# A third seven-product group in the second layer's feed-forward part, with its weight sums made during the first layer's

## The chip, the cores and the metric

The kernel runs on one core of one Trainium2 chip. The metric is the device time of one execution in microseconds; three executions of the kernel before took 783.09, 784.54 and 783.81 us, with a median of 783.81 us. The profile is of a further execution that took 783.19 us.

## The reference

The program is a decoder of two layers over 256 tokens of width 1024, in float32. Layer 0 mixes tokens by a short gated convolution, layer 1 by block-sparse attention on one shared set of keys and values; both then attend to a memory of 256 rows, and both end in a gated feed-forward part of width 2816. That part is what the change is about:

```
D_FF = ((8 * D_MODEL + 3 * 256 - 1) // (3 * 256)) * 256   # 2816

def swiglu(h, w_gu, w_down):
    g, u = jnp.split(h @ w_gu, 2, axis=-1)
    return (jax.nn.silu(g) * u) @ w_down

# in each layer, h of 256 x 1024:
x = x + swiglu(rms_norm(x, norm_ffn), w_gu, w_down)
```

## The kernel before

**Weights.** All matrix products are float32 made of two rounded halves: a weight chunk of 512 KB arrives as `raw_...`, ScalarE rounds it to `hi_...` (the hi split), VectorE subtracts that from the chunk to make `lo_...` (the lo split), and TensorE (`mm3`) forms lo x hi, hi x hi and hi x lo. The chunks have one fixed order, the plan of 278 loads. `RAWS = 5`: a load is issued on SyncE's queue as soon as the chunk five places before it has its lo split. `WBUFS = 10`: ten split chunks may stand ready or in use.

**The feed-forward part.** The 2816 columns are 11 pairs `jp` of 256. Pairs 0 and 1 are made another way. A plain pair loads two gate chunks `wg{l}_{jp}`, two up chunks `wu{l}_{jp}` and the two chunks of down weights `wd{l}_{k}` of the pair two places back. TensorE forms gate and up in PSUM (`gu`) for half of the tokens, ScalarE and VectorE evict them (COPY and addition into `gu_sb`, SiLU, product) into `guT`, and TensorE adds the down products of the earlier pair into `ff`; then the second half of the tokens follows. The stages that the prediction speaks of in layer 0 are pair 6, whose stage uses wd0_8 and wd0_9, and pair 7 with wd0_10 and wd0_11.

**A group** (`seven`) makes two pairs at once. Gate and up of two pairs are seen as a 2 x 2 block of matrices, and seven products of blocks take the place of eight. The products read, in this order, B11, B21, the sums T1, T4, T2, then B22 and T3, two chunks each, with the down products of the earlier pairs put in between. The evictions of the products combine them: B11 by a ScalarE COPY into `m1`; B21 by a VectorE addition into `g0`, then SiLU on ScalarE; T1 by a ScalarE COPY into `p5` and a VectorE subtraction in `m1`; T4, T2, B22 and T3 by VectorE. The result lies with tokens on partitions and is turned by eight transposes (`turn_parts4`, PSUM tile `pt_g`), four for each half of the tokens, the second four while the stage behind the group is running.

**The sums.** T1 to T4 are sums of weight blocks, made in DRAM ahead of their use: for each chunk a copy on SyncE's queue and an accumulating transfer issued by GpSimd (`sum_steps`, eight copies and eight accumulates a group). Their place is given by load numbers: a sum step is issued just before the load of that number. [...]

**What sets the order.** The order of instructions on ScalarE and VectorE is set when the program is built, by a model of a clock. Each time TensorE's work reaches a poll, `poll` takes the open evictions whose inputs the model holds ready, and `pump` issues the next hi or lo split if its engine and its input are free by the model. Loads, copies and accumulates are all charged to one DMA clock, 3300 ns for an accumulate and 1460 for a copy, and a chunk counts as landed by this clock. Once built, the order is fixed: an engine that waits for one instruction doesn't do the next one.

`GROUPS` (L46) lists the first pair of each group by layer, and L47 the load numbers for the sums: first, end and last for each layer. The hooks that put them in are at L1041 to L1046.

```
GROUPS = ((8,), (4, 8))
SUMS_AT = ((44, 104, 104), (128, 220, 210))
```

## Time and profile before

| | |
|---|---|
| median of three runs | 783.81 us |
| the profiled execution | 783.19 us |
| its span | 781.4 us, 11230 instructions |
| granted clock of TensorE, mean | 0.998 |
| lo splits of down chunks on VectorE | 44 x 1.219 us |
| hi splits of down chunks on ScalarE | 44 x 1.050 us |
| read from HBM, written | 178.82 MB, 28.31 MB |

The page gives busy time by engine, then the span in 40 slices, the DMA queues, the chain of work that ended last, the costliest groups of instructions and the DMA issues. Where it names times in a row of the timeline, the first number is the start in us from the span's start and the second the duration; a row that ends in `x4` puts four like instructions together, and brackets hold the idle time ahead of it and what ended that. A row of the windows has the stretch, its length, the busy time of TensorE's matmuls (with the count), of its weight loads, VectorE, ScalarE and GpSimd, then TensorE's granted clock, the busy share of the DMA engines and GB/s.

### The profile page before, as it was taken

What the parts mean: (1) busy time and instruction counts of PE and PEld (TensorE: products, weight loads), DVE (VectorE), ACT (ScalarE), POOL (GpSimd) and SP (SyncE); (2) the same over time, 40 slices, a digit from 0 to 9 for tenths busy, and PEclk for the clock granted to TensorE, in tenths of its full rate; (3) what the DMA queues carried; (4) which work ended last, traced back from release to release, by engine and by line L of the source; (5) the groups of instructions that cost most, each with busy time, mean ns of one, the idle gap of its engine ahead of it and who ended that gap; (6) DMA issues with size and microseconds to landing.
All of it is one profiled execution on the core that took longest, in us unless ns stands there. A gap on an engine that the chain in (4) does not pass through costs nothing.

```text
span 781.4 us, 11230 instructions
## 1 busy us (share of the span) xinstructions
PE 773.5 (99%) x4147; PEld 664.8 (85%) x4147; DVE 574.0 (73%) x872; ACT 459.0 (59%) x728; POOL 39.1 (5%) x68
## 2 busy tenths in 40 slices
PE   9999999999999999999999999999999999999996
PEld 8988888898888888888888889888988888888885
DVE  6988887768785566688756566876867876966964
ACT  7875666665654555566654563655756556655741
POOL 1000011000100000000100010020001000000000
PEclk9999999999999999999999999999999999999999
DMA  9876888926676755699788466889975646946921
GB/s 343 299 259 212 272 292 267 336 65 212 188 247 235 223 177 204 206 367 346 211 251 295 178 161 210 302 239 300 247 209 166 240 159 216 330 165 210 348 107 54
DMA packets 53415, 182.71 MB, mean 234 GB/s; under 512 B 6256, under 2 KB 7280, under 8 KB 52720
## 3 DMA queue, kind: packets, MB, share of 16 engines
q1 hardware_dynamic: 45968, 166.79, 60.0%
q0 software_dynamic: 6816, 14.68, 10.4%
q8 instruction: 32, 0.52, 0.3%
q10 hardware_dynamic: 576, 0.52, 0.2%
q14 instruction: 23, 0.19, 0.1%
HBM read 178.82 MB, written 28.31 MB: 265 GB/s over the span
## 4 chain that ended last, share of the span: by engine, by line
PE 98%; DVE 1%; issue 0%; ACT 0%; POOLq 0%; DVEq 0%; ACTq 0%
PE gu L464 17%; PE ff L464 15%; PE seven L464 7%; PE acc_memk L464 6%; PE q_acc L464 6%; PE cu L464 6%; PE rows L464 6%; PE acc_mo L464 6%; PE acc_memv L464 6%; PE pb L464 3%; PE acc_v L464 3%; PE acc_q L464 3%; PE acc_o L464 3%; PE acc_cout L464 3%; PE acc_k L464 3%; PE po L464 2%
## 5 line engine op out<-in xcount | busy, mean ns | idle before, releaser
L464 PE MATMUL ff<-hi_wd,guT 128*128 128x512 f32 (+1 forms) x352 | 108.3, 388 | 0.0
L464 PEld LDWEIGHTS ff<-hi_wd,guT 128*128 128x128 f32 x352 | 65.8, 188 | 12.8
L464 PE MATMUL ff<-lo_wd,guT 128*128 128x512 f32 (+1 forms) x176 | 68.3, 388 | 0.0
L242 DVE TENSOR_TENSOR gu_sb<-gu_sb,gu 128x256 f32<-128x256 f32 x48 | 19.9, 420 | 57.5 <-ACT gu_sb L242 57.0
L242 DVE TENSOR_TENSOR lo_wd<-raw_wd,hi_wd 128x1024 fp32r<-128x1024 f32 x44 | 53.4, 1219 | 3.7 <-ACT hi_wd L242 3.6
L242 ACT COPY gu_sb<-gu 128x256 f32<-128x256 f32 x48 | 17.8, 373 | 60.0 <-PE gu L464 59.6
L242 ACT CAST hi_wd<-raw_wd 128x1024 fp32r<-128x1024 f32 x44 | 46.1, 1050 | 11.3 <-DMA raw_wd<-in_chunks_dram 11.0
L464 PE MATMUL gu<-ffn,hi_wg 128*128 128x512 f32 x192 | 48.0, 390 | 0.0
L464 PE MATMUL gu<-ffn,hi_wu 128*128 128x512 f32 x192 | 47.6, 390 | 0.0
L464 PE MATMUL acc_memk<-mT,hi_memk 128*128 128x256 f32 x256 | 44.3, 291 | 0.0
L242 ACT CAST hi_wu<-raw_wu 128x1024 fp32r<-128x1024 f32 x32 | 33.6, 1052 | 17.3 <-DMA raw_wu<-in_chunks_dram 12.6
L464 PEld LDWEIGHTS gu<-ffn,hi_wg 128*128 128x128 f32 x192 | 35.9, 188 | 7.3
L464 PEld LDWEIGHTS gu<-ffn,hi_wu 128*128 128x128 f32 x192 | 35.8, 188 | 7.3
L464 PE MATMUL rows<-hi_wr,ffn 128*128 128x512 f32 x128 | 40.7, 395 | 0.0
L464 PE MATMUL acc_mo<-hi_mo,oT_mem 128*128 128x512 f32 x128 | 40.6, 393 | 0.0
L242 DVE TENSOR_TENSOR lo_wu<-raw_wu,hi_wu 128x1024 fp32r<-128x1024 f32 x32 | 38.8, 1219 | 1.3 <-ACT hi_wu L242 1.2
L464 PE MATMUL acc_memv<-hi_memv,mT 128*128 128x512 f32 x128 | 39.6, 390 | 0.0
L464 PEld LDWEIGHTS acc_memk<-mT,hi_memk 128*128 128x128 f32 x256 | 38.7, 197 | 0.6 <-ACT hi_memk L242 0.4
L464 PEld LDWEIGHTS ff<-lo_wd,guT 128*128 128x128 f32 x176 | 33.2, 188 | 6.3
L551 POOL DMA_DIRECT2D T<-in_chunks_dram x24 | 21.9, 913 | 271.4 <-issue 92.1
L242 POOL TENSOR_TENSOR rs<-ms,neg_half 128x1 f32<-128x1 f32 x14 | 13.4, 960 | 395.5 <-DVE ms L242 386.3
L464 PE MATMUL q_acc<-mem,hi_mq 128*128 128x512 f32 x128 | 32.4, 394 | 0.0
(277 smaller groups left out, 1963.8 us busy)
## 6 DMA issues: line engine op xcount, KB each, us to landing
raw_wd<-in_chunks_dram SPq DMA_DIRECT2D x44, 512.0 KB, 5.1
raw_wu<-in_chunks_dram SPq DMA_DIRECT2D x32, 512.0 KB, 5.0
T<-in_chunks_dram POOLq DMA_DIRECT2D x24, 512.0 KB, 8.6
raw_wg<-in_chunks_dram SPq DMA_DIRECT2D x24, 512.0 KB, 5.2
raw_wT<-T SPq DMA_DIRECT2D x24, 512.0 KB, 4.8
raw_wB<-in_chunks_dram SPq DMA_DIRECT2D x18, 512.0 KB, 4.8
raw_memv<-in_chunks_dram SPq DMA_DIRECT2D x16, 512.0 KB, 5.0
raw_mq<-in_chunks_dram SPq DMA_DIRECT2D x16, 512.0 KB, 5.1
```

The costliest lines, as they stand in the source:

```text
L242: return call(out, *args, **kw)
L464: nc.tensor.matmul(o, l, r, start=start, stop=stop)
L551: nc.gpsimd.dma_start(dst, src, accum_op=OP.add, max_dma_last_dim=2048)
```

## The change

There are three groups in layer 1 instead of two, at pairs 3 and 4, 6 and 7, 8 and 9 (before: 4 and 5, 8 and 9). Pairs 2, 5 and 10 stay plain. The last two groups follow each other with no plain pair between them. The plan grows from 278 to 284 loads, since a group reads 14 chunks where two pairs read 8. TensorE's matmuls go from 4103 to 4067.

A group that starts at an odd pair has its two pairs in two different units of `guT`, so `turn_parts4` puts its four turned columns into two units, by two shorter COPYs and subtractions each instead of one.

The places of the sums are now listed by hand, one load number for each step. The sums of layer 0's group (8) stay where they were, and those of layer 1's groups 6 and 8 stand at the numbers that groups 4 and 8 had. New are the sums of group 3, at loads 94 to 116: in layer 0's feed-forward part, from the load of wd0_6 to that of wT4_0_8_0.

The descriptor space goes from 1024 to 2048 bytes a partition; the room comes from `junk` and `blank`, which have one buffer instead of two.

```diff
-GROUPS = ((8,), (4, 8))
-SUMS_AT = ((44, 104, 104), (128, 220, 210))
+GROUPS = ((8,), (3, 6, 8))
+SUMS_AT = {
+    (0, 8): (44, 47, 51, 55, 59, 62, 66, 70, 74, 77, 81, 85, 89, 92, 96, 100),
+    (1, 3): (94, 95, 97, 98, 100, 101, 107, 108, 103, 104, 106, 107, 111, 112, 115, 116),
...
+}
...
-        junk = small.tile([P, 512], BF16, tag="junk", name="junk", bufs=2)
+        junk = small.tile([P, 512], BF16, tag="junk", name="junk", bufs=1)
...
-        steps = [step for jp in GROUPS[l] for step in sum_steps(l, jp)]
-        first, end, last = SUMS_AT[l]
-        for n, step in enumerate(steps):
-            at = min(first + (end - first) * n // len(steps), last + n - len(steps))
-            feed.hooks.setdefault(at, []).append(step)
+        for jp in GROUPS[l]:
+            for at, step in zip(SUMS_AT[l, jp], sum_steps(l, jp)):
+                feed.hooks.setdefault(at, []).append(step)
...
-                yield from split_steps(u[:, :, 0, tok(h)], u[:, :, 1, tok(h)], pt)
+                if j0 == 0:
+                    yield from split_steps(u[:, :, 0, tok(h)], u[:, :, 1, tok(h)], pt)
+                    return
+                for i, v in enumerate((u, unit_of(2 * jp + 2)[0])):
+                    c, q = slice(2 - 2 * i, 4 - 2 * i), pt[:, 2 * i:2 * i + 2, :]
+                    scalar.copy(v[:, c, 0, tok(h)], q)
+                    yield
+                    vector.tensor_sub(v[:, c, 1, tok(h)], q, v[:, c, 0, tok(h)])
+                side.give("tp")
+                yield
...
-                guT.add_job(h, jp // 2, bank_jobs[name])
+                for g in sorted({jp // 2, (jp + 1) // 2}):
+                    guT.add_job(h, g, bank_jobs[name])
...
-    nc = bacc.Bacc("TRN2", target_bir_lowering=False, num_devices=1, dynamic_dma_scratch_size=1024)
+    nc = bacc.Bacc("TRN2", target_bir_lowering=False, num_devices=1, dynamic_dma_scratch_size=2048)
```

The change moves instructions in layer 0 too, where nothing of the computation is changed. Line numbers of the changed kernel are 5 higher there (L247 for L242).

The first place is ScalarE's queue around the hi split of wd0_9, in layer 0's pair 6. Before, it stands ahead of all evictions of that pair; `gu_3092` and `gu_3104` are gate and up of pair 5's second half, and pair 6's gate product is `gu_3160`.

```order
L242 COPY gu_sb0_3090<-gu_3092 128x256
L242 CAST hi_wd0_8_3129<-raw_wd0_8_3022 128x1024
L242 COPY gu_sb1_3091<-gu_3104 128x256
L242 ACTIVATE gu_sb0_3090<-gu_sb0_3090 128x256
L242 CAST hi_wd0_9_3146<-raw_wd0_9_3033 128x1024
L242 CAST guT0_2_2858<-gu_sb1_3091 128x256
L242 CAST hi_wg0_7_0_3165<-raw_wg0_7_0_3044 128x1024
L242 CAST hi_wg0_7_1_3175<-raw_wg0_7_1_3056 128x1024
L242 CAST hi_wu0_7_0_3187<-raw_wu0_7_0_3095 128x1024
L242 CAST hi_wu0_7_1_3207<-raw_wu0_7_1_3153 128x1024
L242 COPY gu_sb0_3158<-gu_3160 128x256
```

In the changed kernel ScalarE has this order there; `gu_3171` and `gu_3183` are gate and up of pair 6's first half, which TensorE forms just before it uses wd0_8 and wd0_9.

```order
L247 CAST hi_wd0_8_3165<-raw_wd0_8_3035 128x1024
L247 COPY gu_sb0_3169<-gu_3171 128x256
L247 CAST hi_wd0_9_3208<-raw_wd0_9_3044 128x1024
L247 COPY gu_sb1_3170<-gu_3183 128x256
L247 ACTIVATE gu_sb0_3169<-gu_sb0_3169 128x256
```

The hi split of wd0_9 has moved behind the COPY of pair 6's own gate product, and the chunks of pair 7, which were split ahead of that COPY, follow later.

The second place is the same queue one pair later, around the hi split of wd0_11. Before, `gu_3241` and `gu_3253` are gate and up of pair 6's second half, so that this split too stands a half stage and more ahead of pair 7's evictions.

```order
L242 COPY gu_sb0_3239<-gu_3241 128x256
L242 CAST hi_wd0_10_3278<-raw_wd0_10_3171 128x1024
L242 COPY gu_sb1_3240<-gu_3253 128x256
L242 ACTIVATE gu_sb0_3239<-gu_sb0_3239 128x256
L242 CAST hi_wd0_11_3295<-raw_wd0_11_3182 128x1024
```

In the changed kernel `gu_3320` and `gu_3329` are gate and up of pair 7's first half.

```order
L247 CAST hi_wd0_10_3331<-raw_wd0_10_3216 128x1024
L247 COPY gu_sb0_3318<-gu_3320 128x256
L247 COPY gu_sb1_3319<-gu_3329 128x256
L247 CAST hi_wd0_11_3364<-raw_wd0_11_3237 128x1024
L247 ACTIVATE gu_sb0_3318<-gu_sb0_3318 128x256
```

The hi split of wd0_11 now stands behind both COPYs of pair 7's first half, whose products TensorE forms just before it uses wd0_10 and wd0_11.

The third place is layer 0's group, on VectorE: `lo_w...` are lo splits, and the rows with `seven` are the evictions of B21 (into `g0`), T1 and T2 (into `m1`) and T4 (into `p5`). Before:

```order
L242 TENSOR_TENSOR lo_wT1_0_8_0_3461<-raw_wT1_0_8_0_3341,hi_wT1_0_8_0_3460 128x1024
L242 TENSOR_TENSOR lo_wT1_0_8_1_3471<-raw_wT1_0_8_1_3353,hi_wT1_0_8_1_3470 128x1024
L242 TENSOR_TENSOR lo_wT4_0_8_0_3482<-raw_wT4_0_8_0_3392,hi_wT4_0_8_0_3481 128x1024
L242 TENSOR_TENSOR lo_wT4_0_8_1_3502<-raw_wT4_0_8_1_3450,hi_wT4_0_8_1_3501 128x1024
L242 TENSOR_TENSOR lo_wT2_0_8_0_3509<-raw_wT2_0_8_0_3466,hi_wT2_0_8_0_3508 128x1024
L242 TENSOR_TENSOR g0_3526<-seven_3495,m1_3484 128x512
```

And in the changed kernel:

```order
L247 TENSOR_TENSOR lo_wT1_0_8_0_3510<-raw_wT1_0_8_0_3417,hi_wT1_0_8_0_3509 128x1024
L247 TENSOR_TENSOR g0_3523<-seven_3501,m1_3487 128x512
L247 TENSOR_TENSOR lo_wT1_0_8_1_3540<-raw_wT1_0_8_1_3461,hi_wT1_0_8_1_3539 128x1024
L247 TENSOR_TENSOR m1_3487<-seven_3532,m1_3487 128x512
L247 TENSOR_TENSOR lo_wT4_0_8_0_3561<-raw_wT4_0_8_0_3475,hi_wT4_0_8_0_3560 128x1024
...
L247 TENSOR_TENSOR lo_wd0_15_3614<-raw_wd0_15_3565,hi_wd0_15_3613 128x1024
L247 TENSOR_TENSOR m1_3487<-seven_3607,m1_3487 128x512
L247 TENSOR_TENSOR lo_wB22_0_8_0_3627<-raw_wB22_0_8_0_3580,hi_wB22_0_8_0_3626 128x1024
```

The eviction of B21 stood behind five lo splits of sums and now stands between the two of T1; the evictions of T1 and T2 now stand just ahead of the lo splits of wT4_0_8_0 and wB22_0_8_0.

ScalarE's queue shows the same in the changed kernel; `m1`, `g0` and `p5` are the COPY of B11, the SiLU on B21's sum and the COPY of T1.

```order
L247 CAST hi_wB21_0_8_0_3482<-raw_wB21_0_8_0_3369 128x1024
L247 COPY m1_3487<-seven_3467 128x512
L247 CAST hi_wB21_0_8_1_3497<-raw_wB21_0_8_1_3403 128x1024
L247 CAST hi_wT1_0_8_0_3509<-raw_wT1_0_8_0_3417 128x1024
L247 ACTIVATE g0_3523<-g0_3523 128x512
L247 CAST hi_wT1_0_8_1_3539<-raw_wT1_0_8_1_3461 128x1024
L247 COPY p5_3551<-seven_3532 128x512
L247 CAST hi_wT4_0_8_0_3560<-raw_wT4_0_8_0_3475 128x1024
```

Before, the hi splits of these chunks (of wB21 the second, of T1 both, of T4 the first) all stand ahead of that COPY of B11:

```order
L242 CAST hi_wB21_0_8_1_3443<-raw_wB21_0_8_1_3330 128x1024
L242 CAST guT0_3_3157<-gu_sb1_3388 128x256
L242 CAST hi_wT1_0_8_0_3460<-raw_wT1_0_8_0_3341 128x1024
L242 CAST hi_wT1_0_8_1_3470<-raw_wT1_0_8_1_3353 128x1024
L242 CAST hi_wT4_0_8_0_3481<-raw_wT4_0_8_0_3392 128x1024
L242 COPY m1_3484<-seven_3455 128x512
```

Each of the four hi splits after the first row has changed places with an eviction of the same group.

## The prediction

> **What bounds the kernel now.** The page comes first: how busy each engine is, which clock was granted, what the DMA queues carried, and the chain of work that ended last.

> ```profile
> PE   773.5 (99%) x4147; PEld 664.8 (85%) x4147; DVE 574.0 (73%) x872; ACT 459.0 (59%) x728; POOL 39.1 (5%) x68
> ...
> PEclk9999999999999999999999999999999999999999
> ...
> q1 hardware_dynamic: 45968, 166.79, 60.0%
> q0 software_dynamic: 6816, 14.68, 10.4%
> ...
> PE 98%; DVE 1%; issue 0%; ACT 0%; POOLq 0%; DVEq 0%; ACTq 0%
> ...
> raw_wd<-in_chunks_dram SPq DMA_DIRECT2D x44, 512.0 KB, 5.1
> ...
> T<-in_chunks_dram POOLq DMA_DIRECT2D x24, 512.0 KB, 8.6
> ```

> TensorE is busy in 773.5 of 781.4 us, at full clock in every slice, and makes up 98% of the chain. So only two things move the time much: matrix work that is added or removed, and stalls of TensorE where today there are none. VectorE (73%) and ScalarE (59%) have room on average, yet every weight chunk passes both of them (the hi split on ScalarE, then the lo split on VectorE) before TensorE may use it. A split that comes too late is the way in which this kernel can lose.

> **Part 1: the third group on TensorE.** The window view below cuts layer 1's feed-forward part where TensorE starts each stage: plain jp 3, the group of 4 and 5, plain jp 6, plain jp 7, the group of 8 and 9.

> ```profile
> 634.91:651.48 16.57, 16.57 (x89) 14.35 (x88) 10.10 (x15) 8.52 (x15) 0.00 (x0) 1.00 0.58 191
> 651.48:682.34 30.86, 30.86 (x138) 25.18 (x136) 28.53 (x31) 22.27 (x25) 0.00 (x0) 1.00 0.92 318
> 682.34:699.40 17.06, 17.06 (x94) 14.74 (x92) 9.79 (x14) 7.93 (x15) 0.00 (x0) 1.00 0.49 164
> 699.40:715.97 16.57, 16.57 (x89) 14.35 (x88) 10.05 (x15) 8.47 (x15) 0.00 (x0) 1.00 0.55 190
> 715.97:746.83 30.86, 30.86 (x137) 25.18 (x136) 28.47 (x31) 22.26 (x25) 0.00 (x0) 1.00 0.91 321
> ```

> Two plain pairs take 2 x 16.57 = 33.14 us, a group 30.86 us. Its result needs turning by eight transposes, four of which fall into the stage behind it: 17.06 instead of 16.57, 0.49 us. One more group thus saves 33.14 - 30.86 - 0.49 = **1.79 us**. This is sure as far as the group stays bound by TensorE, as both present ones do (busy 30.86 of 30.86).

> Two groups now stand back to back. VectorE is busy 28.5 of a group's 30.86 us, ScalarE 22.3, the DMA engines 0.91 to 0.92. A second group behind the first needs the same again, and the first one's last turning, some 1 us of VectorE; 2.3 us are free in each. I charge nothing; the cover is thin, and rival C prices its loss. The single unit that an odd group start now splits over two units costs two short ScalarE copies and two short VectorE subtractions for one long one each, a fraction of a microsecond off TensorE's path: nothing. [...]

> **Part 2: what the eight new sums do to the order in layer 0.** This is the term that decides. The planner charges each copy and accumulate to its DMA clock, so from the load of wd0_6 on it believes the next chunks to land later. It therefore hands ScalarE and VectorE the evictions first and the splits behind them, and the engines run in that order even if the chunk has long landed. The pieces of order shown above have the places: an eviction waits for the end of a TensorE product, and the split queued behind it feeds the matmuls that come almost directly after that product. Before, these splits were far ahead. The timelines of the three engines show it for wd0_9:

> ```profile
> 291.20 1.22 DVE L242 TENSOR_TENSOR lo_wd<-raw_wd,hi_wd 128x1024 fp32r<-128x1024 f32 x1
> ...
> 295.52 0.37 ACT L242 COPY gu_sb<-gu 128x256 f32<-128x256 f32 x1 [0.24 <-PE gu L464]
> ...
> 296.93 0.40 PE L464 MATMUL ff<-lo_wd,guT 128*128 128x512 f32 x1
> ...
> 329.94 1.05 ACT L242 CAST hi_wT<-raw_wT 128x1024 fp32r<-128x1024 f32 x1 [1.41 <-DMA raw_wT<-T]
> ...
> 331.02 1.23 DVE L242 TENSOR_TENSOR lo_wT<-raw_wT,hi_wT 128x1024 fp32r<-128x1024 f32 x1 [0.91 <-ACT hi_wT L242]
> ...
> 335.95 0.58 ACT L242 COPY p<-seven 128x512 f32<-128x512 f32 x1
> 336.43 2.00 ACT L242 CAST hi_wB<-raw_wB 128x1024 fp32r<-128x1024 f32 x2
> ```

> The lo split of wd0_9 ended at 292.42, 4.5 us ahead of its use at 296.93. Two steps are read here for all chains. From the start of a hi split to the end of its lo split: 329.94 to 331.02 + 1.23, **2.31 us**. And ScalarE starts the next operation 0.10 us before a COPY's recorded end (335.95 + 0.58 against 336.43), so 0.27 us after the start of a 0.37 us COPY and 0.48 after that of a 0.58 us one.

> All times below are on the clock of the old trace; a stall moves what follows, but the distance from a product to the use behind it stays, so the stalls add up.

> (1) wd0_9 now stands behind the COPY of its own stage's gate product, which starts at 295.52. Hi split from 295.79, lo done 298.10, use 296.93: **1.17 us**.

> (2) wd0_11 stands behind both COPYs of its stage, the second reading the up product:

> ```profile
> 295.27 1.12 PE L464 MATMUL gu<-ffn,lo_wu 128*128 128x256 f32 x8
> ...
> 296.49 0.37 ACT L242 COPY gu_sb<-gu 128x256 f32<-128x256 f32 x1 [0.59 <-PE gu L464]
> ...
> 311.84 1.12 PE L464 MATMUL gu<-ffn,lo_wu 128*128 128x256 f32 x8
> ...
> 313.50 0.40 PE L464 MATMUL ff<-lo_wd,guT 128*128 128x512 f32 x1
> ```

> In the stage before, that COPY starts 1.22 us after the first of the product's last eight matmuls. Here: 311.84 + 1.22 = 313.06, hi from 313.33, lo done 315.64, use 313.50: **2.14 us**.

> (3) wB21_0_8_1 stands behind the COPY of product B11, (4) wT1_0_8_1 behind the SiLU of product B21, which itself waits for VectorE's addition, and (5) wT4_0_8_0 behind the COPY of product T1, (6) wB22_0_8_0 on VectorE alone behind the addition that reads T2.

> ```profile
> 326.76 0.59 ACT L242 COPY m<-seven 128x512 f32<-128x512 f32 x1 [0.37 <-PE seven L464]
> ...
> 334.49 0.63 ACT L242 ACTIVATE g<-g 128x512 f32<-128x512 f32 x1
> 335.02 1.03 ACT L242 CAST hi_wd<-raw_wd 128x1024 fp32r<-128x1024 f32 x1
> ...
> 343.70 0.68 DVE L242 TENSOR_TENSOR m<-seven,m 128x512 f32<-128x512 f32 x1
> 344.31 1.22 DVE L242 TENSOR_TENSOR lo_wg<-raw_wg,hi_wg 128x1024 fp32r<-128x1024 f32 x1
> ```

> ```profile
> 326.10 0.62 PE L464 MATMUL seven<-hi_wB,ffn 128*128 128x512 f32 x2
> ...
> 329.28 0.39 PE L464 MATMUL seven<-lo_wB,ffn 128*128 128x512 f32 x1
> ...
> 330.18 0.62 PE L464 MATMUL seven<-hi_wB,ffn 128*128 128x512 f32 x2
> ...
> 333.41 0.39 PE L464 MATMUL seven<-lo_wT,S 128*128 128x512 f32 x1
> ...
> 334.34 0.63 PE L464 MATMUL seven<-hi_wT,S 128*128 128x512 f32 x2
> ...
> 336.19 0.40 PE L464 MATMUL seven<-lo_wT,ffn 128*128 128x512 f32 x1
> ...
> 342.63 0.63 PE L464 MATMUL seven<-hi_wT,S 128*128 128x512 f32 x2
> ...
> 343.79 0.39 PE L464 MATMUL ff<-lo_wd,guT 128*128 128x512 f32 x1
> ...
> 344.48 0.40 PE L464 MATMUL seven<-lo_wB,S 128*128 128x512 f32 x1
> ```

> (3) COPY 326.76, hi 327.24, lo done 329.55, use 329.28: **0.27**. (4) B21 ends at 330.80; an eviction starts about 0.05 behind a product's recorded end (B11: 326.10 + 0.62 against 326.76), so the addition runs 330.85 to 331.53, the SiLU starts at 331.58, the hi split 0.53 later at 332.11, lo done 334.42, use 333.41: **1.01**. (5) T1 ends at 334.97, COPY 335.02, hi 335.50, lo done 337.81, use 336.19: **1.62**. (6) T2 ends at 343.26, addition 343.31, the next operation 0.61 later at 343.92, lo done 345.14, use 344.48: **0.66**.

> Together 1.17 + 2.14 + 0.27 + 1.01 + 1.62 + 0.66 = **6.87 us** of new stalls. Bounds: if the present lead of several microseconds survived in some way, 0; if the hi split also started a whole eviction later at each place, by 0.4 to 0.7 us, about 10. I take the sum as it stands, since every step has its own row.

> **The sum.** -1.79 + 6.87 = +5.08 us. The profiled execution took 783.19 us, so the like would take 788.3; against the median of 783.81 it is 788.9. I say **788.6 us**.

> **Rivals.** A, the other side: not slower. The new order may not bind, because the evictions finish earlier against the product than I read (matmul ends are modelled in this profile). Against the median the change is no longer slower by 0.2%, which is what a measurement of this kernel can tell from no change (1.57 us), once the six stalls sum to less than 1.79 + 1.57 = 3.36 us, half of mine; each would have to be about 0.6 us shorter. With none at all the gain alone remains: 783.81 - 1.79 = 782.0, just past that bound. For it speaks that no stall of this kind is in the old trace; against it that the starts of the COPYs are measured. Chance 0.16, of which 0.06 is for faster.

> B: the chunks really land late. A queue's share of the span gives the price of a transfer: q0 10.4% of 781.4 us over 24 accumulates, at most 3.4 us each; q1 60.0% over 166.79 MB, 1.47 us for 512 KB. Eight copies and eight accumulates are 8 x 4.87 = 39 us of DMA time, between the loads of wd0_6 and the group's. There the windows show:

> ```profile
> 300.00:315.00 15.00, 15.00 (x83) 13.04 (x82) 8.66 (x13) 8.52 (x14) 0.00 (x0) 1.00 0.52 175
> 315.00:330.00 15.00, 15.00 (x76) 12.71 (x75) 9.76 (x12) 7.71 (x12) 0.00 (x0) 1.00 0.52 178
> 330.00:345.00 15.00, 15.00 (x67) 12.21 (x66) 12.64 (x14) 10.09 (x11) 0.00 (x0) 1.00 0.97 340
> ```

> Half of the time is free until 330, then nothing. A load takes the buffer of the chunk five places before it, so wd0_15 can now be issued only when lo_wT4_0 is done, at TensorE's stall of place (5); from there to its first use TensorE has about 7.6 us of work (336.19 to 343.79), and landing 5.1 plus splits 2.31 need 7.4. A landing as long as that of an accumulate, 8.6 us, would cost up to 3.5 us. In the forecast I take 0, by the nearest row, the median landing of 5.1; this rival adds 2 to 4: 791 to 793. Chance 0.18. [...]

> C: the two groups back to back run out of VectorE or DMA (28.5 of 30.86 and 0.92 above). Price: the shortfall of one turning and one late chunk, 1 to 3 us, 789.6 to 791.6. Chance 0.07.

> **How the numbers follow.** My forecast 0.59 (787 to 790.5), A 0.16, B 0.18, C 0.07. The range 785.0 to 793.0 leaves out most of A and the far end of B. Faster than 782.2: 0.06; between 782.2 and 785.4: 0.11; above: 0.83.

> **What would show it.** In the new trace TensorE should wait, at weight loads or matmuls, for VectorE's lo splits of wd0_9, wd0_11, wT1_0_8_1, wT4_0_8_0 and wB22_0_8_0, some 7 us in all, and nowhere else in such amounts; ScalarE should be idle ahead of the COPYs in front of those splits, with the chunks landed. Layer 1's feed-forward part should be 1.8 us shorter with TensorE busy throughout. I am wrong in mechanism if these waits end on a DMA, or if layer 0 takes as long as before.

## The result and the profile after

The changed kernel took 792.22 us in the median of five runs (790.75 to 793.95), against 783.38 us before in the same comparison: 1.12% slower, ratio 1.0112 with a 95% interval of 1.0093 to 1.0130. The profile is of the fastest of the five: 790.75 us with a span of 789.0 us, 7.6 us more than the span before.

From the page of the changed kernel come the busy times and the chain, in the same columns as before:

```profile
PE   773.9 (98%) x4111; PEld 661.2 (84%) x4111; DVE 582.0 (74%) x875; ACT 464.6 (59%) x726; POOL 45.6 (6%) x76
...
PE 90%; DMA 4%; DVE 3%; ACT 2%; issue 1%; POOL 0%; SPq 0%; POOLq 0%; DVEq 0%; ACTq 0%
```

(The page's counts of matmuls, 4147 and now 4111, lie 44 above those named with the change; the difference of 36 is the same.) TensorE was 98% of the chain and is 90% now; DMA, VectorE and ScalarE have taken the rest. The view of waits says what TensorE waited for (total, times, longest):

```profile
PE ff L469 <- DVE lo_wd L247: 3.1, 2, 2.0
PE seven L469 <- DVE lo_wT L247: 2.4, 2, 1.5
PE warm L469 <- DVE blank L768: 1.5, 1, 1.5
PE ff L469 <- ACT guT L247: 0.8, 1, 0.8
PE seven L469 <- DVE lo_wB L247: 0.7, 2, 0.5
```

Only the third row was there before. Two waits for lo splits of down chunks, two of sums, two of plain blocks: these are the six places of the prediction, by kind and count. The fourth row is new and was not foreseen. It lies at the end of layer 0's feed-forward part, where ScalarE has an eviction (`guT`) behind the split of a chunk that lands late:

```profile
380.17 1.15 ACT L247 ACTIVATE hi_k<-raw_k,g_cols 128x1024 fp32r<-128x1024 f32 x1 [1.91 <-DMA raw_k<-in_chunks_dram]
381.22 0.39 ACT L247 CAST guT<-gu_sb 128x256 fp32r<-128x256 f32 x1
...
381.66 0.50 PE L469 MATMUL ff<-lo_wd,guT 128*128 128x512 f32 x1 [0.83 <-ACT guT L247]
```

Place (2) in the timelines of ScalarE, VectorE and TensorE of the changed kernel (start, duration, what; idle time ahead in brackets):

```profile
314.80 0.37 ACT L247 COPY gu_sb<-gu 128x256 f32<-128x256 f32 x1 [0.59 <-PE gu L469]
315.06 1.05 ACT L247 CAST hi_wd<-raw_wd 128x1024 fp32r<-128x1024 f32 x1
...
316.15 1.23 DVE L247 TENSOR_TENSOR lo_wd<-raw_wd,hi_wd 128x1024 fp32r<-128x1024 f32 x1 [1.48 <-ACT hi_wd L247]
...
317.43 0.50 PE L469 MATMUL ff<-lo_wd,guT 128*128 128x512 f32 x1 [2.03 <-DVE lo_wd L247]
```

The four steps of the chain are there one behind the other: the COPY that waits for the up product, the hi split of wd0_11, its lo split, and the matmul that has waited 2.03 us for it. No bracket names a DMA at the splits; the chunk was issued at 300.59 and had landed at 307.12 us, eight microseconds before ScalarE touched it.

For each place the delay can be read from the two traces: how much later than before the first matmul with that chunk starts, less the same for the matmul just ahead.

| place | chunk | forecast, us | measured, us |
|---|---|---|---|
| 1 | wd0_9 | 1.17 | 1.2 |
| 2 | wd0_11 | 2.14 | 2.2 |
| 3 | wB21_0_8_1 | 0.27 | 0.3 |
| 4 | wT1_0_8_1 | 1.01 | 1.0 |
| 5 | wT4_0_8_0 | 1.62 | 1.7 |
| 6 | wB22_0_8_0 | 0.66 | 0.7 |
| | sum | 6.87 | 7.1 |

The stalls cost a little more than these delays. The first matmul behind such a wait is recorded with 0.50 us instead of 0.40, and the next one starts 0.34 us behind it instead of 0.23, so that some 0.1 us more is lost at each place. Ahead of place (1) the changed kernel is 0.3 us behind the old one, behind place (6) 8.3 us: the six places cost 7.9 us.

The gain is there as well. These two windows of the changed kernel are its last two groups, back to back:

```profile
692.10:722.96 30.86, 30.86 (x138) 25.19 (x137) 28.53 (x31) 22.10 (x25) 0.00 (x0) 1.00 0.90 317
722.96:753.80 30.84, 30.84 (x139) 25.17 (x138) 27.94 (x30) 21.48 (x24) 0.00 (x0) 1.00 0.91 317
```

TensorE is busy for every microsecond, and a group takes 30.84 to 30.86 us as before. Ahead of layer 1's feed-forward groups the changed kernel is 9.27 us behind the old one, at TensorE's last matmul 7.42: the third group brought 1.85 us.

So the two traces add up: 0.3 us ahead of place (1), at a wait for `q` in the memory attention, 7.9 at the six places, 1.0 between place (6) and layer 1's groups, where the wait for `guT` is, less 1.85 for the group, and 0.2 behind the last matmul make the 7.6 us of the spans. The median of the five runs is not explained by this: it lies 1.5 us above the profiled run, and 3.6 us above the forecast.

### The profile page after: what moved, and what is told of

The parts are those of the page before. It is cut to its first block, busy times and chain, and to the rows that moved or that the text cites. A ratio compares the mean times of both kernels' runs of the same rounds, so it can differ in the third digit from the quotient of the medians.

```text
span 789.0 us, 11206 instructions
## 1 busy us (share of the span) xinstructions
PE 773.9 (98%) x4111; PEld 661.2 (84%) x4111; DVE 582.0 (74%) x875; ACT 464.6 (59%) x726; POOL 45.6 (6%) x76
## 4 chain that ended last, share of the span: by engine, by line
PE 90%; DMA 4%; DVE 3%; ACT 2%; issue 1%; POOL 0%; SPq 0%; POOLq 0%; DVEq 0%; ACTq 0%
PE gu L469 13%; PE ff L469 12%; PE seven L469 9%; PE acc_memk L469 6%; PE cu L469 6%; PE rows L469 6%; PE acc_mo L469 6%; PE q_acc L469 5%; PE acc_memv L469 5%; PE pb L469 3%; PE acc_v L469 3%; PE acc_k L469 3%; PE acc_q L469 3%; PE acc_cout L469 3%; PE acc_o L469 3%; PE po L469 2%
## 5 line engine op out<-in xcount | busy, mean ns | idle before, releaser
L247 DVE TENSOR_TENSOR lo_wd<-raw_wd,hi_wd 128x1024 fp32r<-128x1024 f32 x44 | 53.4, 1221 | 9.6 <-ACT hi_wd L247 9.3
L247 ACT CAST hi_wd<-raw_wd 128x1024 fp32r<-128x1024 f32 x44 | 46.1, 1050 | 9.9 <-DMA raw_wd<-in_chunks_dram 9.0
L247 DVE TENSOR_TENSOR gu_sb<-gu_sb,gu 128x256 f32<-128x256 f32 x40 | 16.4, 419 | 45.7 <-ACT gu_sb L247 45.6
L247 ACT COPY gu_sb<-gu 128x256 f32<-128x256 f32 x40 | 14.8, 373 | 55.5 <-PE gu L469 55.3
L556 POOL DMA_DIRECT2D T<-in_chunks_dram x32 | 29.0, 978 | 237.7 <-DMA T<-T 164.2
L247 DVE TENSOR_TENSOR lo_wT<-raw_wT,hi_wT 128x1024 fp32r<-128x1024 f32 x32 | 38.1, 1220 | 5.4 <-ACT hi_wT L247 5.2
L469 PE MATMUL gu<-ffn,hi_wg 128*128 128x512 f32 x160 | 39.9, 390 | 0.0
L469 PE MATMUL gu<-ffn,hi_wu 128*128 128x512 f32 x160 | 39.6, 390 | 0.0
L247 ACT CAST hi_wT<-raw_wT 128x1024 fp32r<-128x1024 f32 x32 | 32.8, 1051 | 9.7 <-DMA raw_wT<-T 8.4
L247 POOL TENSOR_TENSOR rs<-ms,neg_half 128x1 f32<-128x1 f32 x14 | 12.6, 898 | 427.6 <-DVE ms L247 418.2
L247 ACT CAST hi_wu<-raw_wu 128x1024 fp32r<-128x1024 f32 x28 | 29.3, 1050 | 12.3 <-DMA raw_wu<-in_chunks_dram 7.4
L469 PEld LDWEIGHTS gu<-ffn,hi_wg 128*128 128x128 f32 x160 | 29.8, 188 | 6.1
L247 DVE TENSOR_TENSOR lo_wu<-raw_wu,hi_wu 128x1024 fp32r<-128x1024 f32 x28 | 33.9, 1219 | 1.5 <-ACT hi_wu L247 1.4
## 6 DMA issues: line engine op xcount, KB each, us to landing
raw_wd<-in_chunks_dram SPq DMA_DIRECT2D x44, 512.0 KB, 5.5
T<-in_chunks_dram POOLq DMA_DIRECT2D x32, 512.0 KB, 9.6
raw_wT<-T SPq DMA_DIRECT2D x32, 512.0 KB, 4.7
raw_wu<-in_chunks_dram SPq DMA_DIRECT2D x28, 512.0 KB, 5.7
raw_wB<-in_chunks_dram SPq DMA_DIRECT2D x24, 512.0 KB, 5.0
raw_wg<-in_chunks_dram SPq DMA_DIRECT2D x20, 512.0 KB, 5.6
raw_memv<-in_chunks_dram SPq DMA_DIRECT2D x16, 512.0 KB, 5.0
T<-in_chunks_dram SPq DMA_DIRECT2D x16, 512.0 KB, 7.0
```

What stands on the lines that cost most here:

```text
L247: return call(out, *args, **kw)
L469: nc.tensor.matmul(o, l, r, start=start, stop=stop)
L556: nc.gpsimd.dma_start(dst, src, accum_op=OP.add, max_dma_last_dim=2048)
```

## The experiments

Two theories were set against each other: the **order theory** (the loss is made by the order that the planner gives because of the charges) and the **transfer theory** (it is made by chunks that land late beside the sums). The planner allows a clean cut: the charge and the transfer are two statements.

**The transfers without the charge.** The changed kernel, with these edits in `sum_steps`:

```diff
-                clock.free["dma"] = max(clock.free["dma"], clock.now)
+                if (l, jp) != (1, 3):
+                    clock.free["dma"] = max(clock.free["dma"], clock.now)
...
-                clock.note("dma", 3300 if add else 1460, [], [])
+                if (l, jp) != (1, 3):
+                    clock.note("dma", 3300 if add else 1460, [], [])
```

> The changed kernel with group 3's sixteen sum steps no longer charged to the planner's DMA clock; the transfers are issued at the same loads as before, so their real load on the DMA engines stays. The order on ScalarE, VectorE and TensorE up to layer 1's feed-forward part is then that of the kernel before. Order theory (the loss is made by the order that the charges produce): the six stalls go, the group's gain stays: 783.4 - 1.8 = 781.6 us, and TensorE waits for splits in layer 0 by less than 1 us. Transfer theory (the loss is made by chunks that land late beside the sums): the loss stays, 788 to 793 us, with ScalarE and then TensorE waiting for chunks in layer 0.

Measured: 785.38 us (784.14 to 787.68), ratio 1.0025 [1.0013, 1.0037] to before. Most of the loss is gone, but the run is 3.8 us above the 781.6 of the order theory, so neither theory has it alone. ScalarE, VectorE and TensorE have the order of the old trace here, up to layer 1's feed-forward part. The timelines of ScalarE and TensorE in this run show the largest part of what the transfers cost:

```profile
300.73 1.04 ACT L247 CAST hi_wu<-raw_wu 128x1024 fp32r<-128x1024 f32 x1 [5.64 <-DMA raw_wu<-in_chunks_dram]
301.68 0.64 ACT L247 COPY gu_sb<-gu 128x256 f32<-128x256 f32 x2
...
302.55 2.11 PE L469 MATMUL gu<-ffn,hi_wg 128*128 128x512 f32 x8 [1.57 <-DVE gu_sb L247]
```

Here the old order hurts. ScalarE waits 5.64 us for a chunk (wu0_7_1, the same wait was 0.99 us before), and the evictions stand behind that split. So TensorE finds no free `gu` buffer and waits 1.57 us, for a chunk that it needs only 11 us later. It is the mirror image of the six places: there a split stood behind an eviction that waited for TensorE, here an eviction behind a split that waits for a DMA. Against the old trace TensorE stands 1.9 us later behind this wait than ahead of it. Another 0.6 us go at an earlier wait for `gu`, at 284 us, and 0.9 us at the memory attention's `q`, at 151 us, which the third experiment takes up.

**The charge without the transfers.** The kernel before, with the sixteen charges at the same load numbers, and neither a third group nor its transfers:

```diff
+    def charge(add):
+        def run():
+            clock.free["dma"] = max(clock.free["dma"], clock.now)
+            clock.note("dma", 3300 if add else 1460, [], [])
+        return run
+
+    for at, add in zip((94, 95, 97, 98, 100, 101, 107, 108, 103, 104, 106, 107, 111, 112, 115, 116),
+                       (0, 0, 0, 0, 1, 1, 1, 1, 0, 0, 1, 1, 0, 0, 1, 1)):
+        feed.hooks.setdefault(at, []).append(charge(add))
```

> The kernel before, with the sixteen charges to the planner's DMA clock at loads 94 to 116 and nothing else: no further group, no further transfer. The order in layer 0 is then that of the changed kernel. Order theory: 783.4 + 6.9 of stalls at the six places, plus the wait of 0.8 us for guT that the changed kernel's trace shows behind them: 790.3 to 791.2 us. Transfer theory: 783.4 us, at most 1 us more.

Measured: 792.45 us (791.23 to 793.45), ratio 1.0111 [1.0094, 1.0128]. A kernel that computes and transfers exactly what the old one does is 9 us slower, by a list of numbers that only the planner sees. The transfer theory falls as the main cause. The waits of this run are the six again:

```profile
PE ff L464 <- DVE lo_wd L242: 3.1, 2, 2.0
PE seven L464 <- DVE lo_wT L242: 2.3, 2, 1.5
...
PE seven L464 <- DVE lo_wB L242: 0.7, 2, 0.5
```

But 9 us is more than the 7.9 that these places give. Its windows show where the rest is (the last three columns are TensorE's granted clock, the DMA share and GB/s):

```profile
310.00:318.00 8.00, 5.97 (x34) 4.99 (x33) 3.03 (x4) 2.01 (x4) 0.00 (x0) 1.00 0.42 131
318.00:326.00 8.00, 8.00 (x33) 6.52 (x32) 3.21 (x4) 3.25 (x4) 0.00 (x0) 0.79 0.61 195
```

The first window holds the wait of place (2): 5.97 of 8 us busy. In the second TensorE is busy throughout, but at a granted clock of 0.79, and gets through 33 matmuls. Against the first profile of the changed kernel, which has the same order here, it lost another 1.6 us there without waiting for anything. Of the four runs, the one of 791.23 us has a mean granted clock of 0.999 and lies 7.8 us above the kernel before; that of 792.14 us has 0.996, the profiled one of 792.75 us 0.995, and the one of 793.45 us 0.997, which does not tell. (The mean has the half clock of the last microseconds in it, 3.0 us in the trace of the kernel before and 4.5 in the first one of the changed kernel; the runs of the kernel before, whose trace has no fall ahead of that, show 0.997 to 0.999.)

**The ring and the junk buffer alone**, in the kernel before:

```diff
-        junk = small.tile([P, 512], BF16, tag="junk", name="junk", bufs=2)
+        junk = small.tile([P, 512], BF16, tag="junk", name="junk", bufs=1)
...
-    nc = bacc.Bacc("TRN2", target_bir_lowering=False, num_devices=1, dynamic_dma_scratch_size=1024)
+    nc = bacc.Bacc("TRN2", target_bir_lowering=False, num_devices=1, dynamic_dma_scratch_size=2048)
```

> The kernel before with 2048 instead of 1024 bytes of descriptor space and with one junk buffer instead of two, nothing else. Both theories: 783.4 us, within 0.2%. If the ring or the junk buffer carried the loss, 785 us or more.

Measured: 784.27 us (783.78 to 784.79), ratio 1.0010 [1.0001, 1.0020]: inside the 0.2% that I had named, but not nothing. GpSimd's timeline shows how. Before:

```profile
126.41 1.06 POOL L551 DMA_DIRECT2D T<-in_chunks_dram  x1
132.35 0.91 POOL L551 DMA_DIRECT2D T<-in_chunks_dram  x1 [4.88 <-issue]
141.34 0.89 POOL L551 DMA_DIRECT2D T<-in_chunks_dram  x1 [8.08 <-issue]
```

And with the larger ring and one junk buffer:

```profile
126.58 2.89 POOL L551 DMA_DIRECT2D T<-in_chunks_dram  x3
142.81 0.90 POOL L551 DMA_DIRECT2D T<-in_chunks_dram  x1 [13.34 <-DMA T<-in_chunks_dram]
```

Three accumulates of layer 0's sums go out in 2.89 us instead of some 16 us. In the old kernel no two of the 24 accumulates are in flight together; in the first profile of the changed one up to three are. The three loads of chunks that SyncE issues next, beside two or three accumulates, land after 7.1, 8.2 and 9.9 us instead of 5.3, 5.0 and 5.1. About 24 us behind the accumulates TensorE waits 0.5 us for a `q` in the memory attention, where it did not before, and stands about 1 us later behind this wait than ahead of it.

**Both together**: no charge, and the old ring and buffers (the first edit, and the third taken back).

> As the first of this set (no charge for group 3's sums), but with the old 1024 bytes of descriptor space and two junk buffers. One accumulate less is in flight, so the accumulates of group 3 end later. Order theory: the same as the first within 0.5 us, about 781.6 us, if the sums still end ahead of the loads that read them. Transfer theory: as bad as the changed kernel or worse, 790 us or more, since GpSimd's queue is served one transfer at a time and SyncE's copies wait for it.

Measured: 785.75 us (784.58 to 789.64), ratio 1.0040 [1.0024, 1.0055]. That is no better than with the new ring, and the runs are wider apart. Their mean granted clocks go with the times: 0.995 and 0.996 in the two at 789.6 us, 0.996 at 787.9, 0.997 at 787.0, and 0.998 or 0.999 in the six that took up to 785.8 us. The order theory's 781.6 is missed as in the first run, and the transfer theory's 790 too. The wait for a free `gu` buffer is there again, with all of it at one place:

```profile
PE gu L469 <- DVE gu_sb L247: 2.1, 1, 2.1
```

So the old ring alone doesn't help sums that are packed into 22 loads.

**Half of the charges.** If it is the order, the loss must not follow the charged time but the places, which can be read from the built program. The kernel before with only the first eight charges of the second experiment:

> The kernel before with only the first eight of the sixteen charges (copies and accumulates of T1 and T3, loads 94 to 108), no further group and no further transfer. In the order that this gives, only place (1) has a split behind the eviction of its own stage (wd0_9 behind the gate COPY); wd0_11 and the group's splits stand ahead of theirs. Order theory, by places: 783.4 + 1.2 = 784.6 us, with one wait for wd0_9. A theory in which the charged time itself counts (eight of sixteen charges, 19 of 38 us on the planner's clock) would give about half of the 9 us that all sixteen cost, 788 us.

And with only the last eight:

> The kernel before with only the last eight charges (T2 and T4, loads 103 to 116). In this order none of the six splits stands behind the eviction that held it: 783.4 us by places, within 0.2%. By the share of charged time: about 788 us.

Measured: 784.50 us (784.24 to 785.50), ratio 1.0016 [1.0007, 1.0025], and 783.90 us (783.15 to 785.64), ratio 1.0010 [1.0000, 1.0019]. In the first, TensorE has the one wait that the places give, and the second has none at all in this part:

```profile
PE ff L464 <- DVE lo_wd L242: 1.1, 1, 1.1
```

The two halves cost 1.1 and 0.5 us, and the whole 9: the loss is made by which split ends up behind which eviction, and not by an amount of charge.

**One split put back.** The changed kernel, where the planner may issue one hi split without its own landing time. This moves the hi and lo split of wd0_11 ahead of the evictions of place (2) and nothing else on any engine:

```diff
-            if self.clock.ready(self.raw[n]) <= now + SLACK:
+            if self.clock.ready(self.raw[n]) <= now + SLACK or self.items[n]["name"] == "wd0_11":
```

> The changed kernel with one edit: the planner may issue the hi split of wd0_11 without its own landing time, which moves this split and its lo split ahead of the two evictions of place (2) and moves nothing else on any engine. Order theory with a stall alone: the 2.14 us of place (2) go, 792.2 - 2.1 = 790.1 us. If TensorE's clock sometimes falls behind this longest stall (as the trace with the charges alone shows, 0.79 in 318 to 326 us), the fall goes too: 788.3 to 789 us, and the runs lie closer together. Transfer theory: no change, 792 us.

Measured: 788.62 us (788.21 to 789.97), ratio 1.0070 [1.0057, 1.0082]. Two instructions moved by a place or two, and the median falls by 3.6 us, 1.5 more than the stall of 2.14 that they made. This is what was expected if the clock falls behind this stall in some runs (788.3 to 789 us), and not the stall alone (790.1). The mean granted clock is 0.998 or 0.999 in all five runs, against 0.995 to 0.997 in those of the changed kernel. The profile, of this kernel's slowest run, has the other waits still:

```profile
PE seven L469 <- DVE lo_wT L247: 2.4, 2, 1.5
...
PE ff L469 <- ACT guT L247: 1.5, 1, 1.5
PE ff L469 <- DVE lo_wd L247: 1.1, 1, 1.1
```

**The changed kernel once more**, for a second profile.

> The changed kernel once more, for a second profile. Its five times lie between 790.8 and 794.0 us, and the profile of the fastest shows no stretch with a lower clock. If falls of TensorE's clock behind the 2-us wait make the difference between its runs, a run of 792 us or more has a stretch of some microseconds with a granted clock well under 1 behind that wait, a run of 791 us has none. A spread from late chunks would show as longer waits for DMAs instead.

Measured: 793.86 us, one run. Its windows around place (2):

```profile
314.00:320.00 6.00, 3.97 (x26) 3.29 (x25) 2.41 (x4) 2.01 (x4) 0.88 (x1) 1.00 0.63 199
320.00:326.00 6.00, 6.00 (x21) 4.78 (x20) 2.79 (x3) 3.25 (x4) 0.90 (x1) 0.72 1.06 220
326.00:332.00 6.00, 6.00 (x36) 5.28 (x35) 2.67 (x5) 2.91 (x6) 0.00 (x0) 1.00 0.58 201
```

In the first profile of the same kernel the middle window is this:

```profile
320.00:326.00 6.00, 6.00 (x36) 5.28 (x35) 2.60 (x4) 2.47 (x5) 0.00 (x0) 1.00 1.07 273
```

The same wait of 2.0 us, the same engine full, 21 matmuls in place of 36 at a clock of 0.72. Of the 3.1 us between the two runs this is 1.6; another 1.5 us are lost by 155 us, about half of them at the memory attention's `q`, where the old kernel with the new ring and junk buffer waits too, and most of the others at a weight split near 25 us. Narrower windows show that the 0.72 is a clock of one half for 3.4 us:

```profile
317.00:320.40 3.40, 1.37 (x6) 1.04 (x6) 1.99 (x3) 1.56 (x4) 0.88 (x1) 1.00 0.74 187
320.50:323.80 3.30, 3.30 (x9) 2.56 (x8) 2.75 (x3) 2.77 (x3) 0.90 (x1) 0.50 1.06 243
323.90:327.30 3.40, 3.40 (x19) 2.91 (x18) 0.00 (x0) 0.00 (x0) 0.00 (x0) 1.00 1.06 235
```

So the wait of place (2) is sometimes followed by a lower clock and sometimes not, and the traces show a difference. The time from the clock's first rise to full to its fall is a whole multiple of 3.413 us: 226 of these intervals in the kernel before (771.41 us, to the fall at the program's end), 228 in the first profile of the changed kernel (778.24 us, to the same), and here it rises at 6.44 us and falls at 320.46, which is 92 intervals later. Three traces have a fall ahead of the program's end: this one and the one with the charges alone, both after 92 intervals, and that of the last experiment below, after 127. In the interval just ahead of it TensorE was idle for 2.03, 2.02 and 2.40 us. In no interval between the first rise and the last matmul was it idle for more than 0.08 us in the kernel before and 1.50 in the first profile of the changed kernel, and the longest wait of the first experiment, 1.57 us, had a clock of 1.00 behind it. In the first profile of the changed kernel the same wait of 2.03 us lies across the end of an interval, 1.47 us in one and 0.56 in the next, and the clock stayed full.

**The sums spread out.** If the rest of the loss comes from sixteen transfers within 22 loads, spreading them must take it away. The changed kernel without the charge, with the old ring and buffers, and T1 and T3 a little further apart, T2 and T4 much later, in layer 1's attention:

```diff
-    (1, 3): (94, 95, 97, 98, 100, 101, 107, 108, 103, 104, 106, 107, 111, 112, 115, 116),
+    (1, 3): (99, 101, 103, 105, 102, 104, 106, 108, 157, 158, 160, 161, 176, 177, 179, 180),
```

> The changed kernel with the sums of group 3 spread out: T1 and T3 at loads 99 to 108, T2 and T4 at 157 to 180, none of them charged to the planner's clock, 1024 bytes of descriptor space and two junk buffers. The order up to layer 1's feed-forward part is that of the kernel before. If the loss that is left without the charge (785.4 us instead of 781.6) comes from chunks that land late beside sixteen transfers packed into 22 loads, spreading them takes it away: 781.6 to 782.4 us, a little faster than before. If it comes from anything else, it stays at 785 us.

Measured: 781.98 us (781.28 to 782.52), ratio 0.9982 [0.9973, 0.9991]. It beats both kernels, by 1.4 us the one before and by 10.2 us the changed one, and has most of the group's 1.8 us. From the kernel with no charge and the old ring, at 785.75 us, it differs in the places of the sums alone. Its waits of TensorE, all of them:

```profile
PE warm L469 <- DVE blank L770: 1.5, 1, 1.5
PE pt L473 <- DVE p L247: 0.7, 1, 0.7
PE acc_memk L469 <- DVE lo_memk L247: 0.4, 1, 0.4
```

**The same with the change's ring and junk buffer**, to see what they do to the good version.

> The version with the spread sums, but with the change's 2048 bytes of descriptor space and one junk buffer. If the 0.87 us that these two cost the kernel before come from GpSimd issuing three accumulates at once at 126 us (seen in that trace), the same loss appears here: 782.0 + 0.9 = 782.9 us, and the wait for q ahead of the memory attention's scores is there again. If a larger ring helped the sums of group 3, 781.6 us or less.

Measured: 787.93 us (787.05 to 789.20), ratio 1.0062 [1.0046, 1.0079]. I had the sign right and the size wrong: 5.9 us instead of 0.9, and at another place than expected. GpSimd and ScalarE in this run:

```profile
421.65 0.88 POOL L557 DMA_DIRECT2D T<-in_chunks_dram  x1 [9.85 <-DMA T<-T]
424.12 0.90 POOL L557 DMA_DIRECT2D T<-in_chunks_dram  x1 [1.59 <-DMA T<-T]
424.77 0.85 POOL L1656 DMA_DIRECT2D mT<-mem_aside  x1
...
434.35 1.15 ACT L247 ACTIVATE hi_v<-raw_v,g_cols 128x1024 fp32r<-128x1024 f32 x1 [3.06 <-DMA raw_v<-in_chunks_dram]
435.41 0.67 ACT L247 ACTIVATE r<-acc_q,rs 128x512 f32<-128x512 f32 x1
```

With the old ring the second accumulate waited until 436.35. Here it goes out at 424.12, with the transfer of `mT` right behind it and a microsecond and a half ahead of the load of v1_7, which takes 8.6 us to land instead of 3.4. ScalarE waits for that chunk 3.06 us with the eviction `r` behind it, and TensorE needs `r`. Its wait and its clock:

```profile
PE pt_r L473 <- DVE r L247: 2.5, 1, 2.5
```

```profile
434.00:440.00 6.00, 3.53 (x16) 2.69 (x16) 2.98 (x9) 4.82 (x6) 0.00 (x0) 0.85 0.94 387
440.00:446.00 6.00, 6.00 (x27) 4.92 (x26) 3.46 (x8) 2.29 (x7) 0.00 (x0) 0.87 0.65 239
```

The mirrored stall again, of 2.5 us, and with it again a clock of one half for 3.4 us, here across the two windows; the mean granted clock is 0.995 or 0.996 in all four runs. Of the 5.9 us the two kernels' traces show 4.6, with 3.5 at this place. Which of the two, the ring or the single junk buffer, costs how much wasn't tried apart. The traces show accumulates issued closer together; that this is the ring's doing is my reading of them.

## Why the prediction was right, and where it was short

**Direction and range.** Slower was forecast with 0.83 and 785.0 to 793.0 us; it is slower, at 792.22. The forecast of 788.6 was 3.6 us short.

**Part 1**, -1.79 us: right. The third group brings 1.85 us in the traces, TensorE is busy throughout the two groups that stand back to back, and rival C did not come about.

**Part 2**, the six places: right in mechanism, in place and in the length of each stall (6.87 forecast, 7.1 measured), and shown to be the order alone by the kernel that has the charges and nothing else. What was mis-sized is what these stalls cost: with the slower start behind each they take 7.9 us, and the order alone measured 9.0. I read the clock as full in every slice of the old trace and then reckoned the new stalls at that clock. It held behind the shorter stalls: the windows behind those of up to 1.5 us show 1.00. Behind the 2.03 us of place (2) it fell to one half for 3.4 us in two of three profiled runs, at a cost of 1.6 us each time, and taking that one stall out brought 1.5 us more than the stall.

**The ring and the junk buffer** have no term in the sum, and in the old kernel they cost 0.9 us. The traces show three accumulates that go out together, in 2.89 us, and loads beside them that land 2 to 5 us later.

**Rival B**, late chunks, was partly true. Chunks did land late: without the charge, transfers and ring cost 3.8 us, 0.9 of it at `q`. But not where the rival put it. The wait that they add to the changed kernel's trace is the 0.8 us for `guT` at the end of layer 0, which the kernel with the charges alone does not have: ScalarE has the eviction behind splits of chunks that it waits for, by 1.01 and 1.91 us. Together with the new order, sums and ring cost 1.6 us more than the order alone (792.22, against 792.45 less the group's 1.8). **Rival A** fell: the evictions do not finish earlier against the products than the rows say.

The sum as measured in the two traces: -1.85 (group) + 7.9 (the six stalls with the slower start behind each) + 1.0 (around `guT`) + 0.3 (`q`) + 0.2 (behind the last matmul) = 7.6 us. The median of the five runs lies 1.5 us above this. A fall of the clock behind place (2), 1.6 us, and a longer wait for `q` account for such a difference in the second profile; how often each of them came in the five runs is not shown.

## What to carry to other kernels

When a planner orders instructions by a model of transfer times, added background transfers change the program where nothing was edited. Compare the order of instructions of both programs, look for each producer that now stands behind an instruction that waits for the consumer's own last product, and price it from three durations. A wait of 2.0 us cost 3.6 us here where the clock fell behind it. A fixed order on an engine fails in two mirrored ways, a split behind an eviction and an eviction behind a late split; transfers that were spread out and not charged avoided both here, and a limit that happens to spread them was worth keeping (here, by my reading, the small descriptor ring: 781.98 us with it and two junk buffers, 787.93 with the change's).

## What the runs showed of the hardware

GpSimd's accumulates over 512 KB landed in 8.6 us in the median with 1024 bytes of descriptor space, where no two of the 24 are in flight together. In the first experiment, with 2048 bytes, the eight of group 3 took 11.9 us in the median, and the down chunks loaded beside them 6.7 us instead of 4.3 in the same stretch of the old trace. With 1024 bytes (no charge, old ring) the same eight accumulates took 10.3 us.
